# Weight differences and residual adds of a fast-matrix-product FFN stage, moved from GpSimd to VectorE

## The chip, the cores and the metric

The kernel runs on one core of one Trainium2 chip. The metric is the device time of one execution in microseconds (us); each time quoted for a kernel is a median of several runs, and beside it there is one profiled execution with its trace. TensorE runs the matrix products, VectorE (DVE in the rows) and ScalarE (ACT) do elementwise work and can read PSUM, GpSimd (POOL) does elementwise work on SBUF only, SyncE (SP) issues the DMAs. PEld in the rows is TensorE's weight load.

## The reference

One decoder layer: RMS norm, forgetting attention with an output product, a residual add, RMS norm, a SwiGLU feed-forward block, a residual add, and a final RMS norm. What matters here is the end:

```python
def swiglu(h, w_in, w_out):
    gate, up = jnp.split(h @ w_in, 2, axis=-1)
    return ((jax.nn.silu(gate) * up) @ w_out).astype(h.dtype)
...
    h = h + swiglu(rms_norm(h, ffn_norm[i]), ffn_w_in[i], ffn_w_out[i])
h = rms_norm(h, final_norm)
return h[:, N_META:]
```

`h` here is 1024 x 1024 (the 16 meta rows are not needed any more), the hidden width is 2816, and all is float32.

## The kernel before

**The second product of the feed-forward block** (`... @ w_out`) is the last stage. It is a 2 x 2 block product done with seven block products in place of eight (Strassen-Winograd): the hidden activations are cut in four blocks of 512 rows by 1408, the weights `w2` in four blocks of 1408 by 512. The sums of activation blocks (`s1` to `s4`) were made in the stage before by `hidden_sums` and lie in DRAM; the differences of weight blocks are made in this stage, in place:

- t1 = w12 - w11, written over w11 (`to_t1`, line 1015)
- t2 = w22 - t1, written over w11 again (`to_t2`, line 1028)
- t3 = w22 - w12, written over w12 (`to_t3`, line 1036)
- t4 = w21 - t2, written over w21 (`to_t4`, line 1054)

The seven products run in the order a11, a12, s1, s2, s3, s4, a22. Each has 11 steps over the inner dimension (`h` in `prod2`), each step 4 row blocks (`i`), and each of those 3 matmuls (lines 945 to 947): every float32 operand is split into a high and a low part of a format that TensorE takes, and high x high, high x low and low x high are added in PSUM. So a step is 12 matmuls of 128 x 128 by 128 x 512, a product 132.

**What feeds a step.** `left` (line 938) loads the 128 x 512 activation tile by SP's queue into one of four `rm` buffers, and `split` (lines 735 to 740) makes the two parts: ScalarE casts the high part, VectorE subtracts it for the low part. The weight tile is split in the same way. The parts lie in pools `wh` and `wl` of eight buffers each; a step takes two of each, so splits can be four steps ahead of TensorE and no more. `load_w` loads weight tiles, one with each step, put behind the latest `left` load in SP's queue. In s1 to s4 a call `ahead(h)` makes the weight difference of step `h` before its split; the aliases `wt` and `rt` (lines 962 and 963) both are GpSimd's `tensor_tensor`. Of a22's 11 steps the last eight (`TM`) are ordered by row block, with the weight parts in tiles of their own (`t4h` in the buffer of tag `xh`, `t4l`).

**What takes the products away.** `prod2` returns four PSUM banks. They alternate between two sets of four, so a product's banks are wanted again by the product after the next. a11 is copied to `x1` by ScalarE (line 1009) and a12 is added to it by VectorE into `c11` (line 1012); s1 is copied to `p5` by ScalarE (line 1021); s2 is added to `x1`, from then on `u2` (line 1033); s3 + u2 gives `u3` (line 1041); s4 is added to u2 (line 1059); a22 is added to u3 at the very end (line 1082). Residual rows of `h` come from DRAM (`residual`, line 965): a load into one of three `wraw` buffers, then an add on GpSimd (line 968). There are 16 of them, four for each quarter of the output. `square_sum` (line 972, ScalarE) makes the sums for the last norm; GpSimd multiplies c11 and p5 by the gain `gob` (lines 1026 and 1051); `finish` scales and stores.

**Order.** The program is written in the order above, and a planner puts the instructions of each engine in one fixed order at build time from its own simulated times (`schedule_with_timeline_sim=True`): an instruction that is ready and has the earliest place in the program goes first. On the chip each engine keeps that order; an instruction that waits holds what is behind it. SP's queue is in order too.

Of the kernel before, what the change touches and what calls it, by code (L numbers as in the profile page):

```python
# [11 lines left out]
ALU = mybir.AluOpType  # L12
# [3 lines left out]
D = 1024  # L16
# [6 lines left out]
NHP = NHT // 2  # L23
EPS = 1e-6
# [11 lines left out]
def fox_block(ctx, tc, hT, hN, wqkvg, w0f, w0g, wo, w1, w2, g_attn, g_ffn, g_fin, g_q, g_k, b_f, out):  # L36
    nc = tc.nc
# [81 lines left out]
    def t512(tag, name, dt=F32):  # L119
        return ap_.tile([P, 512], dt, tag=tag, name=name, bufs=BUFS[tag])  # L120
# [4 lines left out]
    xh = [xhb[:, k] for k in range(NK)]  # L125
# [609 lines left out]
    def split(src, name):  # L735
        hi = wp.tile([P, 512], F32R, tag="wh", name=f"{name}h", bufs=8)
        lo = wp.tile([P, 512], F32R, tag="wl", name=f"{name}l", bufs=8)
        nc.scalar.copy(hi, src)
        nc.vector.tensor_tensor(lo, src, f32v(hi), ALU.subtract)
        return hi, lo  # L740
# [14 lines left out]
    tt = nc.vector.tensor_tensor  # L755
# [134 lines left out]
    def block(tag, name):  # L890
        if tag in ("V", "K"):
            if not spare.get(tag):
                t = ap2.tile([P, 2, 512], F32, tag=tag, name=name, bufs=2)
                spare[tag] = [t[:, 0], t[:, 1]]
            return spare[tag].pop(0)
        return t512(tag, name)

    w11 = [block(g, f"w11_{h}") for h, g in enumerate(["raw"] * 4 + ["tmp"] * 4 + ["V"] * 3)]
    w21 = [block(g, f"w21_{h}") for h, g in enumerate(["sb"] * 8 + ["K"] * 3)]
    wide = {  # L900
        g: big.tile([P, 16, 512], F32, tag=g, name=f"w2{g}")[:, :, :512] for g in ("xh", "xl")
    }
    w12, w22 = ([wide[g][:, h] for h in range(NHP)] for g in ("xh", "xl"))
    x1 = [t512("cmb", f"x1q{i}") for i in range(4)]
    u3 = [wide["xl"][:, NHP + i] for i in range(4)]
    c11, p5 = (
        [v for n in range(2) for v in (lambda t: (t[:, 0], t[:, 1]))(
            ap_.tile([P, 2, 512], F32, tag="Q", name=f"{m}_{n}", bufs=4))]
        for m in ("c11", "p5")
    )  # L910
    gob = [block("K", "go0"), block("V", "go1")]
# [5 lines left out]
    def load_w(blocks, o, d):  # L917

        def go(h):
            def load():  # L920
                nc.sync.dma_start(blocks[h], w2[h + NHP * o, :, 512 * d : 512 * d + 512])

            if queued:
                with tc.issue_after(queued[-1].ins):
                    load()
            else:
                load()

        return go
# [3 lines left out]
    def banks(name):  # L933
        nprod[0] += 1
        tags = ("SSSO", "mmmM")[nprod[0] % 2]
        return [bank(g, f"y{name}_{n}") for n, g in enumerate(tags)]

    def left(name, h):
        g = t512("rm", f"g{name}_{h}")
        queued.append(nc.sync.dma_start(g, gq_d[name][h]))  # L940
        return split(g, f"g{name}_{h}")

    def mm(o, i, h, g, w):
        sl = slice(i * P, (i + 1) * P)
        nc.tensor.matmul(o, lhsT=g[0][:, sl], rhs=w[0], start=(h == 0), stop=False)  # L945
        nc.tensor.matmul(o, lhsT=g[0][:, sl], rhs=w[1], start=False, stop=False)  # L946
        nc.tensor.matmul(o, lhsT=g[1][:, sl], rhs=w[0], start=False, stop=(h == NHP - 1))  # L947

    def prod2(name, n, blocks, upto=NHP, ahead=None, after=None):
        py = banks(n)  # L950
        for h in range(upto):
            g = left(name, h)
            if ahead is not None:
                ahead(h)
            w = split(blocks[h], f"w{n}_{h}")
            for i in range(4):
                mm(py[i], i, h, g, w)
            if after is not None:
                after(h)
        return py  # L960

    wt = nc.gpsimd.tensor_tensor
    rt = nc.gpsimd.tensor_tensor

    def residual(dst, i, c):
        t = wp.tile([P, 512], F32, tag="wraw", name=f"hr{i}_{c}", bufs=3)
        nc.sync.dma_start(t, hd[i, :, 512 * c : 512 * c + 512])
        rt(dst, dst, t, ALU.add)

    def square_sum(ss, c, h, name):  # L970
        sq = t512("cmb", name)
        nc.scalar.activation(sq, h, AF.Square, bias=0.0, scale=1.0, accum_out=ss[:, c : c + 1])

    def sums(i, n):

        shape = [P, NT, 4] if n > 1 else [P, 8]
        t = sm.tile(shape, F32, tag="ssq" if n > 1 else ("ss", "sv", "sr", "sy0")[i], name=f"oss{i}{n}", bufs=2 if n > 1 else 1)
        if n > 1:
            t = t.rearrange("p a b -> p (a b)")
        return t  # L980
# [26 lines left out]
    y = prod2("a11", 1, w11, ahead=load_first)  # L1007
    for i in range(4):
        nc.scalar.copy(x1[i], y[i])
    y = prod2("a12", 2, w21, ahead=load_w(w12, 0, 1))  # L1010
    for i in range(4):
        tt(c11[i], y[i], x1[i], ALU.add)
        residual(c11[i], i, 0)

    def to_t1(h):
        wt(w11[h], w12[h], w11[h], ALU.subtract)
        load_w(w22, 1, 1)(h)

    y = prod2("s1", 5, w11, ahead=to_t1)
    for i in range(4):  # L1020
        nc.scalar.copy(p5[i], y[i])

    ss = sums(0, 4)
    for i in range(4):
# [1 line left out]
        nc.gpsimd.tensor_tensor(c11[i], c11[i], gob[0], ALU.mult)  # L1026

    def to_t2(h):
        wt(w11[h], w22[h], w11[h], ALU.subtract)

    y = prod2("s2", 6, w11, ahead=to_t2)
    for i in range(4):
        tt(x1[i], y[i], x1[i], ALU.add)
    u2 = x1

    def to_t3(h):
        wt(w12[h], w22[h], w12[h], ALU.subtract)

    y = prod2("s3", 7, w12, ahead=to_t3)
    for i in range(4):  # L1040
        tt(u3[i], y[i], u2[i], ALU.add)
        rt(u2[i], u2[i], p5[i], ALU.add)
        residual(u2[i], i, 1)
    for i in range(4):
        rt(p5[i], p5[i], u3[i], ALU.add)
        residual(p5[i], 4 + i, 1)
        residual(u3[i], 4 + i, 0)
    bs = sums(1, 4)
    for i in range(4):
        square_sum(bs, i, p5[i], f"osq{4 + i}_1")  # L1050
        nc.gpsimd.tensor_tensor(p5[i], p5[i], gob[1], ALU.mult)
    nc.vector.tensor_scalar(bs[:, 4:8], bs[:, 0:4], 1.0 / D, EPS, ALU.mult, ALU.add)

    def to_t4(h):
        wt(w21[h], w21[h], w11[h], ALU.subtract)

    y = prod2("s4", 3, w22, ahead=to_t4)
    for i in range(4):
        tt(u2[i], y[i], u2[i], ALU.add)


    TM = 8
    y = prod2("a22", 4, w21, upto=NHP - TM)
    gs, ws = [], []
    his = big.tile([P, 16, 512], F32R, tag="xh", name="t4h")[:, :, :512]
    los = [t512(g, f"t4l{n}", F32R) for n, g in enumerate((["raw"] * 4 + ["tmp"] * 4)[:TM])]
    for n in range(TM):
        h = NHP - TM + n
# [71 lines left out]
```

## Time and profile before

| | |
|---|---|
| time, median of 3 runs | 1428.16 us (1428.06 to 1429.14) |
| the profiled execution: its time | 1425.88 us |
| the profiled execution: its span | 1424.2 us, 20704 instructions |
| busy in the span: TensorE | 1375.4 us, 97% |
| VectorE | 1017.0 us, 71% |
| ScalarE | 661.9 us, 46% |
| GpSimd | 466.6 us, 33% |
| HBM traffic | 124 GB/s over the span |

Times in the profile are microseconds from the start of the span. Busy times of TensorE come from modelled ends of pipelined matmuls, so a gap between two starts shows a stall better than the busy share does. Waits are inferred from semaphore events and put down to the one that came last.

### The profile page before, as it was taken

What the parts mean: (1) busy time and instruction counts of PE and PEld (TensorE: products, weight loads), DVE (VectorE), ACT (ScalarE), POOL (GpSimd) and SP (SyncE); (2) the same over time, 40 slices, a digit from 0 to 9 for tenths busy, and PEclk for the clock granted to TensorE, in tenths of its full rate; (3) what the DMA queues carried; (4) which work ended last, traced back from release to release, by engine and by line L of the source; (5) the groups of instructions that cost most, each with busy time, mean ns of one, the idle gap of its engine ahead of it and who ended that gap; (6) DMA issues with size and microseconds to landing.
All of it is one profiled execution on the core that took longest, in us unless ns stands there. A gap on an engine that the chain in (4) does not pass through costs nothing.

```text
span 1424.2 us, 20704 instructions
## 1 busy us (share of the span) xinstructions
PE 1375.4 (97%) x6699; PEld 1113.3 (78%) x6699; DVE 1017.0 (71%) x1796; ACT 661.9 (46%) x1428; POOL 466.6 (33%) x724
## 2 busy tenths in 40 slices
PE   7999999999999999999997999999999999999997
PEld 7897887878786887866676888888888888876875
DVE  7656776776876777755758786666666765799696
ACT  6455555646565556635435333322233324444534
POOL 4012625244251626244404011111111111598091
PEclk9999999999999999999998999999999999999999
DMA  6353436272625345289773142233333228652344
GB/s 203 103 145 95 138 105 172 77 200 73 185 86 135 109 116 177 81 282 359 276 264 126 60 138 106 94 107 111 111 111 112 97 81 310 218 168 89 97 148 155
DMA packets 118526, 207.18 MB, mean 145 GB/s; under 512 B 18057, under 2 KB 27282, under 8 KB 118418
## 3 DMA queue, kind: packets, MB, share of 16 engines
q1 hardware_dynamic: 118418, 205.86, 45.1%
q8 instruction: 53, 0.87, 0.3%
q14 instruction: 55, 0.45, 0.1%
HBM read 125.71 MB, written 50.60 MB: 124 GB/s over the span
## 4 chain that ended last, share of the span: by engine, by line
PE 72%; DVE 12%; DMA 6%; ACT 4%; issue 3%; SPq 3%; POOL 0%; DVEq 0%; ACTq 0%; POOLq 0%
PE f L750 10%; PE f L752 10%; PE f L751 10%; PE pj L196 5%; PE pj L197 5%; PE pj L198 5%; PE O L413 4%; DMA wraw<-wqkvg 3%; PE y L946 3%; PE y L945 3%; PE y L947 3%; PE S L359 2%; PE S L360 2%; DVE rm L381 2%; ACT sb L402 1%
## 5 line engine op out<-in xcount | busy, mean ns | idle before, releaser
L196 PE MATMUL pj<-wh,xhb 128*128 128x384 f32 (+1 forms) x512 | 176.7, 346 | 6.4 <-ACT xhb L147 5.7
L197 PE MATMUL pj<-wl,xhb 128*128 128x384 f32 (+1 forms) x512 | 175.3, 344 | 0.0
L198 PE MATMUL pj<-wh,xlb 128*128 128x384 f32 (+1 forms) x512 | 173.1, 342 | 0.0
L371 POOL TENSOR_SCALAR_AFFINE_SELECT sb<-sb 128x128 f32<-128x128 f32 (+2 forms) x160 | 54.5, 344 | 339.4 <-ACT sb L366 338.9
L366 ACT ACTIVATE sb<-S,nb 128x512 f32<-128x512 f32 (+4 forms) x224 | 116.3, 540 | 69.8 <-POOL gap L426 35.4
L428 POOL TENSOR_TENSOR t<-t,sb 128x512 f32<-128x512 f32 (+4 forms) x160 | 140.4, 877 | 4.1
L829 POOL TENSOR_TENSOR gs<-u,u 128x512 f32<-128x512 f32 x11 | 14.2, 1292 | 370.9 <-DVE u L816 370.9
L381 DVE TENSOR_TENSOR rm<-rm,sb 128x512 f32<-128x512 f32 (+4 forms) x160 | 103.2, 645 | 36.1 <-POOL sb L371 17.6
L401 DVE TENSOR_TENSOR sb<-sb,pb 128x512 f32<-128x512 f32 (+4 forms) x224 | 95.8, 497 | 35.6 <-PE pb L395 34.1
L402 ACT ACTIVATE sb<-sb 128x512 f32<-128x512 f32 (+4 forms) x224 | 95.2, 482 | 43.8 <-DVE sb L401 43.8
L196 PEld LDWEIGHTS pj<-wh,xhb 128*128 128x128 f32 x512 | 97.6, 191 | 15.6 <-ACT xhb L147 5.7
L197 PEld LDWEIGHTS pj<-wl,xhb 128*128 128x128 f32 x512 | 97.8, 191 | 1.3
L198 PEld LDWEIGHTS pj<-wh,xlb 128*128 128x128 f32 x512 | 97.2, 190 | 1.2
L413 PE MATMUL O<-sb,V 128*64 128x512 f32 (+4 forms) x448 | 94.4, 464 | 1.1 <-ACT sb L402 1.1
L359 PE MATMUL S<-Q,K 128*128 128x512 f32 (+4 forms) x224 | 76.5, 344 | 0.4 <-ACT sb L366 0.4
L360 PE MATMUL S<-Q,K 128*128 128x512 f32 (+4 forms) x224 | 72.5, 328 | 0.0
L413 PEld LDWEIGHTS O<-sb,V 128*64 128x64 f32 (+1 forms) x448 | 32.9, 135 | 35.9 <-issue 20.4
L106 DVE TENSOR_TENSOR wl<-wraw,wh 128x512 fp32r<-128x512 f32 x56 | 43.8, 788 | 22.8 <-ACT wh L104 21.2
L796 DVE TENSOR_TENSOR u<-f,x 128x512 f32<-128x512 f32 x19 | 13.1, 691 | 62.0 <-PE f L752 62.0
L104 ACT CAST wh<-wraw 128x512 fp32r<-128x512 f32 (+1 forms) x64 | 38.6, 607 | 37.9 <-DMA wraw<-wqkvg 26.4
L359 PEld LDWEIGHTS S<-Q,K 128*128 128x128 f32 (+1 forms) x224 | 39.1, 175 | 19.5 <-ACT sb L366 8.0
L451 PE MATMUL pg<-xhb,wh 128*128 128x512 f32 x112 | 45.1, 403 | 0.4 <-DVE tk L308 0.3
(1382 smaller groups left out, 3879.2 us busy)
## 6 DMA issues: line engine op xcount, KB each, us to landing
Q<-tq SPq DMA_DIRECT2D x128, 128.0 KB, 2.3
wraw<-wqkvg SPq DMA_DIRECT2D x56, 256.0 KB, 4.2
av<-w SPq DMA_DIRECT2D x22, 512.0 KB, 3.2
gs<-qs SPq DMA_DIRECT2D x44, 256.0 KB, 2.6
ga<-qa SPq DMA_DIRECT2D x33, 256.0 KB, 3.8
K<-tk SPq DMA_DIRECT2D x64, 128.0 KB, 2.7
wowh<-wod SPq DMA_DIRECT2D x32, 256.0 KB, 5.5
wowl<-wod SPq DMA_DIRECT2D x32, 256.0 KB, 5.7
```

What stands on the lines that cost most here:

```text
L196: nc.tensor.matmul(o, lhsT=xh[k][:, sl], rhs=wh, start=(k == 0), stop=False)
L197: nc.tensor.matmul(o, lhsT=xh[k][:, sl], rhs=wl, start=False, stop=False)
L198: last_mm[0] = nc.tensor.matmul(o, lhsT=xl[k][:, sl], rhs=wh, start=False, stop=(k == NK - 1))
L359: nc.tensor.matmul(psx[:n, s0:], lhsT=kk[:, j * P : j * P + n], rhs=q[:, 0, s0:], start=True, stop=False)
L366: nc.scalar.activation(sj, psx[:n, s:], AF.Identity, bias=nbias[c][:n, j, head : head + 1], scale=1.0)
L381: nc.vector.tensor_tensor(rm[:n, s:], rm[:n, s:], sj, ALU.max)
L402: nc.scalar.activation(sj, sj, AF.Exp, bias=0.0, scale=1.0)
L413: nc.tensor.matmul(po[r, s:], lhsT=st["V"][:n, j, r], rhs=sj, start=(i == 0), stop=(i == nt - 1))
L428: nc.gpsimd.tensor_tensor(total[e][:n, s:], src[:n, s:], sj, ALU.add)
L750: nc.tensor.matmul(pp, lhsT=s[0][:, ks], rhs=bh, start=(k == 0), stop=False)
L751: nc.tensor.matmul(pp, lhsT=s[0][:, ks], rhs=bl, start=False, stop=False)
L752: nc.tensor.matmul(pp, lhsT=s[1][:, ks], rhs=bh, start=False, stop=(k == 3))
```

## The change

All four weight differences go from GpSimd to VectorE (`tt` is VectorE's `tensor_tensor`). `residual` gets a source: the add reads a product from PSUM together with the loaded rows and writes to SBUF, on VectorE. The residual of the first quarter is added to a11 (into c11) and a12 then to that sum; the residuals of the two right-hand quarters are added to s1, in two results: `p5` as before and the new `p5u`, which lies in four free slots of the buffer that holds w12 (rows of 2048 bytes per slot); ScalarE's four copies of s1 go. The add of p5u to u2, of u3 to p5, and of the last residual to u3 go to VectorE and to later places. What stays on GpSimd in this stage are the eight multiplies by `gob`.

```diff
-    wt = nc.gpsimd.tensor_tensor
-    rt = nc.gpsimd.tensor_tensor
-    def residual(dst, i, c):
+    def residual(dst, src, i, c):
         t = wp.tile([P, 512], F32, tag="wraw", name=f"hr{i}_{c}", bufs=3)
         nc.sync.dma_start(t, hd[i, :, 512 * c : 512 * c + 512])
-        rt(dst, dst, t, ALU.add)
+        tt(dst, src, t, ALU.add)
...
     y = prod2("a11", 1, w11, ahead=load_first)
     for i in range(4):
         nc.scalar.copy(x1[i], y[i])
+        residual(c11[i], y[i], i, 0)
     y = prod2("a12", 2, w21, ahead=load_w(w12, 0, 1))
     for i in range(4):
-        tt(c11[i], y[i], x1[i], ALU.add)
-        residual(c11[i], i, 0)
+        tt(c11[i], y[i], c11[i], ALU.add)
     def to_t1(h):
-        wt(w11[h], w12[h], w11[h], ALU.subtract)
+        tt(w11[h], w12[h], w11[h], ALU.subtract)
         load_w(w22, 1, 1)(h)
     y = prod2("s1", 5, w11, ahead=to_t1)
+    p5u = [wide["xh"][:, NHP + i] for i in range(4)]
     for i in range(4):
-        nc.scalar.copy(p5[i], y[i])
+        residual(p5u[i], y[i], i, 1)
+        residual(p5[i], y[i], 4 + i, 1)
...
     def to_t2(h):
-        wt(w11[h], w22[h], w11[h], ALU.subtract)
+        tt(w11[h], w22[h], w11[h], ALU.subtract)
...
     def to_t3(h):
-        wt(w12[h], w22[h], w12[h], ALU.subtract)
+        tt(w12[h], w22[h], w12[h], ALU.subtract)
     y = prod2("s3", 7, w12, ahead=to_t3)
     for i in range(4):
         tt(u3[i], y[i], u2[i], ALU.add)
-        rt(u2[i], u2[i], p5[i], ALU.add)
-        residual(u2[i], i, 1)
+    def to_t4(h):
+        tt(w21[h], w21[h], w11[h], ALU.subtract)
+    y = prod2("s4", 3, w22, ahead=to_t4)
     for i in range(4):
-        rt(p5[i], p5[i], u3[i], ALU.add)
-        residual(p5[i], 4 + i, 1)
-        residual(u3[i], 4 + i, 0)
+        tt(u2[i], u2[i], p5u[i], ALU.add)
+        tt(u2[i], y[i], u2[i], ALU.add)
+    TM = 8
+    y = prod2("a22", 4, w21, upto=NHP - TM)
     bs = sums(1, 4)
     for i in range(4):
+        tt(p5[i], p5[i], u3[i], ALU.add)
+        residual(u3[i], u3[i], 4 + i, 0)
         square_sum(bs, i, p5[i], f"osq{4 + i}_1")
         nc.gpsimd.tensor_tensor(p5[i], p5[i], gob[1], ALU.mult)
...
-    def to_t4(h):
-        wt(w21[h], w21[h], w11[h], ALU.subtract)
-    y = prod2("s4", 3, w22, ahead=to_t4)
-    for i in range(4):
-        tt(u2[i], y[i], u2[i], ALU.add)
-    TM = 8
-    y = prod2("a22", 4, w21, upto=NHP - TM)
```

## Rows read from the trace of the kernel before

**Rows 1.** The page: busy time, share of the span, instructions of each engine.
```profile
PE 1375.4 (97%) x6699; PEld 1113.3 (78%) x6699; DVE 1017.0 (71%) x1796; ACT 661.9 (46%) x1428; POOL 466.6 (33%) x724
```
**Rows 2.** Timeline of TensorE: first matmul of products a12 to a22, and the last.
```profile
1223.52 0.39 PE L945 MATMUL y<-w_0h,ga_0h 128*128 128x512 f32 x1
...
1253.44 0.39 PE L945 MATMUL y<-w_0h,gs_0h 128*128 128x512 f32 x1
...
1286.35 0.39 PE L945 MATMUL y<-w_0h,gs_0h 128*128 128x512 f32 x1
...
1321.71 0.39 PE L945 MATMUL y<-w_0h,gs_0h 128*128 128x512 f32 x1
...
1351.63 1.07 PE L945 MATMUL y<-w_0h,gs_0h 128*128 128x512 f32 x4
...
1383.56 0.39 PE L945 MATMUL y<-w_0h,ga_0h 128*128 128x512 f32 x1
...
1416.73 0.39 PE L947 MATMUL y<-t4h,ga_10l 128*128 128x512 f32 x1
```
**Rows 3.** Windows, one for each product a12 to a22: span, busy us (instructions), clock, DMA.
```profile
1223.52:1253.44 29.92, 29.92 (x134) 24.77 (x132) 23.05 (x23) 13.08 (x25) 17.40 (x13) 1.00 0.60 194
1253.44:1286.35 32.91, 31.45 (x134) 24.39 (x132) 30.66 (x24) 16.25 (x33) 32.91 (x20) 1.00 0.46 144
1286.35:1321.71 35.36, 32.35 (x134) 24.15 (x132) 33.82 (x29) 13.07 (x25) 25.68 (x16) 1.00 0.32 99
1321.71:1351.63 29.92, 29.92 (x134) 24.78 (x132) 20.14 (x33) 16.54 (x31) 0.21 (x1) 1.00 0.31 89
1351.63:1383.56 31.93, 30.83 (x133) 24.52 (x132) 31.93 (x23) 12.88 (x26) 31.93 (x19) 1.00 0.47 146
1383.56:1416.96 33.40, 31.54 (x133) 24.06 (x131) 24.84 (x46) 17.79 (x42) 8.68 (x6) 1.00 0.49 168
```
**Rows 4.** Timeline of TensorE inside a step of s2: what it waited for.
```profile
1306.75 0.39 PE L945 MATMUL y<-w_6h,gs_6h 128*128 128x512 f32 x1
1307.52 0.50 PE L946 MATMUL y<-w_6l,gs_6h 128*128 128x512 f32 x1 [0.39 <-DVE w_6l L739]
```
**Rows 5.** Timeline of VectorE, late in s2.
```profile
1310.79 1.78 DVE L739 TENSOR_TENSOR gs_8l<-gs,gs_8h 128x512 fp32r<-128x512 f32 x1
1312.49 0.68 DVE L739 TENSOR_TENSOR w_8l<-w,w_8h 128x512 fp32r<-128x512 f32 x1
1313.10 0.68 DVE L739 TENSOR_TENSOR gs_9l<-gs,gs_9h 128x512 fp32r<-128x512 f32 x1
```
**Rows 6.** Timeline of GpSimd: its last instructions in s2.
```profile
1303.48 8.55 POOL L1055 TENSOR_TENSOR w<-w,w 128x512 f32<-128x512 f32 x5
```
**Rows 7.** By line: VectorE's adds of a12 from PSUM (min/median/max ns, first and last start).
```profile
L1012 DVE TENSOR_TENSOR c<-y,x1q x4: 675/676/678, 1253.4 to 1256.3; 128x512 f32<-128x512 f32 x4
```
**Rows 8.** Groups of GpSimd by line, 1210 to 1425: count, busy us, mean ns, idle before.
```profile
L1029 POOL TENSOR_TENSOR w<-w2xl,w 128x512 f32<-128x512 f32 x11 | 19.1, 1740 | 0.0
...
L1016 POOL TENSOR_TENSOR w<-w2xh,w 128x512 f32<-128x512 f32 x11 | 16.0, 1469 | 21.1 <-DMA w2xh<-w 17.7 <-DVE w_3l L739 1.6 <-issue 1.0
...
L1026 POOL TENSOR_TENSOR c<-c,w 128x512 f32<-128x512 f32 x4 | 6.9, 1735 | 0.0
```
**Rows 9.** Waits from 1200 us on: us in total, times, longest.
```profile
ACT osq L972 <- POOL c L968: 12.1, 4, 4.8
```
**Rows 10.** Timeline of SP's queue early in s1.
```profile
1253.53 0.32 SPq L940 DMA_DIRECT2D gs<-qs  x1
...
1259.35 0.32 SPq L967 DMA_DIRECT2D hr<-hd  x1
1259.76 0.38 SPq L940 DMA_DIRECT2D gs<-qs  x1
```
**Rows 11.** By line: from issue to landing, residual loads (line 967).
```profile
DMA to landing us min/median/max: 2.6/3.0/6.4
```
**Rows 12.** By line: from issue to landing, weight loads (line 921).
```profile
DMA to landing us min/median/max: 2.6/4.0/6.9
```

## The prediction

> **What bounds the kernel now.** I read the page first: TensorE is busy 97% of the span [rows 1], so only stalls of TensorE are to be had. The change touches the last stage alone, so I went to the timeline of TensorE there and took the first matmul of each product [rows 2]. Products a12 and s3 take 29.92 us each, 132 matmuls at 0.2267 us: TensorE without a stall. The others take longer: s1 32.91 (2.99 over), s2 35.36 (5.44 over), s4 31.93 (2.01 over), and a22 33.40 from its first matmul to 0.23 us behind the start of its last (3.48 over). The sum of the excess is 13.92 us. The clock column is 1.00 in all six windows [rows 3], so this is waiting and not a slower clock.
>
> What it waits for stands inside a step [rows 4]: the first matmul of step 6 of s2 starts at 1306.75, the second only at 1307.52 in place of 1306.98, released by VectorE's low part of the weights. One step of s2 needs two such splits. VectorE starts them 1.70 us apart (1310.79 to 1312.49) and then, from 1312.49 on, 0.61 apart [rows 5]; in between GpSimd's last weight difference ends, at 1303.48 + 8.55 = 1312.03 [rows 6]. So the same instruction on the same kind of tile costs 1.70 us beside GpSimd and 0.60 without it. Two at 1.70 are 3.40 us a step, and TensorE needs 2.72 (29.92 / 11). That is why the excess stands where GpSimd is busy through the window and VectorE too: s1, s2, s4 have GpSimd at 32.91, 25.68, 31.93 us; in s3 it has 0.21 and there is no excess [rows 3]. a22 inherits emptied buffers from s4. In a12 GpSimd works 17.40 us, with breaks, and the buffers hold.
>
> A second path has the same source. The square sums of c11 waited 12.1 us for GpSimd's residual adds [rows 9], and ScalarE's casts stand behind them in its order; SP's queue stood from 1253.53 to 1259.35 until such an add freed a `wraw` buffer, with the next activation load behind it [rows 10].
>
> **The change part by part.**
>
> *GpSimd loses 44 differences and 16 residual adds, and 8 adds of u2 and p5.* What it keeps is 4 + 4 multiplies by the gain (1.735 us each beside VectorE [rows 8]). The gain of this part is bounded by 13.92 us, since TensorE's matmuls stay as they are, 924 of them.
>
> *VectorE takes the 44 differences.* No row shows one on VectorE. The nearest is the split itself, also two SBUF inputs and one output of 128 x 512: 0.60 us pitch alone, 1.70 beside GpSimd [rows 5]; these are the bounds, and I take 0.60 but for what the eight multiplies disturb. The inputs at multiples of 2048 bytes are no other case: the weight tiles that are split in s3 are slots of the same kind, and s3 has VectorE at 20.14 us for 33 instructions with no excess [rows 3]. Each of the products s1 to s4 gets 11 of them: 11 x 0.60 = 6.6 us.
>
> *VectorE takes residual adds and the adds of u2, p5, u3.* With a source in PSUM the bound below is a12's add, 0.676 us, measured while GpSimd was busy [rows 3, 7]: such an add does not slow beside GpSimd. I take 0.60 of pitch for all. Counts per product after the change, old splits included: s1 22 splits + 11 differences + 4 adds = 37; s2 22 + 11 + 8 = 41; s3 37; s4 22 + 11 + 4 + 4 = 41; a22 22 + 12 = 34 and the small work of the norm. At 0.60: 22.2, 24.6, 22.2, 24.6, 20.4 us, each under TensorE's 29.92. a12 has 26 (15.6 us), and differences may move up into it once w12 is there.
>
> *The eight multiplies stay and collide.* Each takes one VectorE instruction from 0.60 to 1.70: 1.1 us, 8.8 us in all, 4.4 in one product. On s2 that is 24.6 + 4.4 = 29.0, still under 29.92 but with nothing to spare. The Trainium skill ("SBUF — State Buffer", section "Who interferes with whom") says that a Vector instruction with two SBUF inputs and a GpSimd one that reads SBUF block each other, the later one wholly; the 1.70 to 0.60 step agrees. By full blocking for GpSimd's 1.735 us the eight would cost 13.9 us.
>
> *The adds that are moved, and the queues.* 16 residual loads remain 16, 0.32 us of SP each [rows 10]; four go ahead of a12's loads, eight from behind s3 to behind s1, past the loads of s2 and s3. They land in 3.0 us [rows 11] and have three buffers: of the eight adds behind s1 three find their rows there, and two more rounds of three each wait for landing and add, about 1.8 + 2 x 3.6 = 9 us. What stands behind them on VectorE are the splits of s2; four steps of finished splits are a cover of 10.9 us. The banks of s1 are held 9 us in place of some 2.5, and are wanted by s3, 29.92 us later: nothing. ScalarE loses four copies that were not on the path: nothing. The buffer of `t4h` now comes free only after u2 + p5u; the eight casts and subtractions that fill it then may gather at the start of a22, where the last eight steps want them 8.2 us (three steps) in.
>
> *A wait that is new.* A difference whose weights come late made GpSimd wait, 17.7 us in line 1016 [rows 8], at no cost. On VectorE such a wait holds the splits. Weight loads land in 4.0 us, 6.9 at most [rows 12]. Bounds: nothing, where the planner puts the difference behind the landing; or up to the spread of 2.9 us at some steps, under the cover of 10.9 as long as it does not recur at each step.
>
> **Sum.** 13.92 us of excess, less what I leave: nothing in s1, s3, s4; 1 us in s2 (29.0 of 29.92 in VectorE, the eight adds); 1 us in a22 (its multiplies, `t4h`). That is 12 us. Of the profiled execution's 1425.88 it leaves 1413.9; the median of the runs is 2.28 us above that execution, so I forecast 1428.16 - 12 = 1416.2 us (-0.84%).
>
> **The rivals.**
>
> *Crowding.* The waits go, but s2 or a22 keeps an excess, because the eight adds stand as one block with their loads or because `t4h`, the splits and u2, u3, p5 gather at the start of a22. For it: 29.0 of 29.92, and a22's 3.48 us today. Against: 74% load over the six products (15.6 + 22.2 + 24.6 + 22.2 + 24.6 + 24 with the norm = 133 of 179.5 us) leaves room to run ahead. Price 3 to 7 us more: about 1420 (1418.5 to 1423).
>
> *The loads hold VectorE.* If 11 differences of t1 and 11 of t3 each wait 1 us more, that is 11 us in each of a12 and s1, beside 15.6 to 24.6 of work: 26.6 to 35.6 against 29.92, and most of the gain is gone: 1425.3 to 1430. For it: line 1016's waits [rows 8]. Against: the loads run a product ahead.
>
> *VectorE becomes the bound: slower.* s1 to s4 hold 156 VectorE instructions in 119.7 us; at a pitch of 0.77 they fill it, and at (119.7 + 13.9) / 156 = 0.86 all of today's excess is back. With the multiplies' 8.8 us I have 0.656. If in-order waits for ScalarE's casts and for loads bring the mean to 0.90, TensorE loses 140.4 - 133.6 = 6.8 us against today: 1435. For it: VectorE is at 93 to 100% of its windows in s1, s2, s4 [rows 3]. Against: that share is made of 1.70s. The Trainium skill ("Perfetto Trace Analysis", section "Optimizing Scalar/DVE Operations") says to move work away from a saturated VectorE, to GpSimd if need be, which would speak for this rival; it adds that the two share a port and that this may not help, and the rows decide for the second.
>
> **Chances.** Forecast 0.60 (its own range 1413.5 to 1418.5), crowding 0.25, loads 0.08, VectorE the bound 0.07. Nothing below 1428.16 - 13.92 = 1414.2 but for the scatter between runs. About 0.2% (2.9 us) is what a measurement of this kernel tells from no change. Faster by more: 0.60 + 0.25 = 0.85; within: 0.08; slower: 0.07. The range takes in the forecast and crowding, 85%: 1413 to 1423.
>
> **What would show it.** In the profile after: splits of s1, s2, s4 at 0.68 us except beside the eight multiplies; GpSimd near empty from a12 on; first matmuls of s2, s3, s4, a22 29.9 us apart; no square sum waiting for GpSimd. Crowding shows as a gap at the second to fourth step of s2 or of the last eight steps of a22; late loads as VectorE idle before a difference, released by a DMA. I would be wrong if a difference on VectorE took clearly over 0.7 us with GpSimd idle, or if the planner set differences or adds ahead of splits that TensorE wants sooner.

## The result and the profile after

The changed kernel takes 1419.28 us (median of 6 runs, 1416.00 to 1424.52), the kernel before 1429.05 beside it (6 runs, 1428.06 to 1432.30): a ratio of 0.9931 [0.9917, 0.9946], 9.8 us less. The forecast was 12 us less, 1416.2; 1419.28 lies in the stated range (1413 to 1423), but above the forecast's own (1413.5 to 1418.5).

The page's busy times, which answer to [rows 1]: GpSimd falls from 466.6 to 361.1 us, and VectorE falls too, from 1017.0 to 995.4, though it has 68 instructions more.

```profile
PE 1372.7 (97%) x6699; PEld 1116.0 (79%) x6699; DVE 995.4 (70%) x1864; ACT 659.9 (47%) x1424; POOL 361.1 (25%) x656
```

The first matmuls of a12, s1, s3, s4 and a22 and the last of all, on TensorE's timeline, answer to [rows 2]; at the seam of s1 and s2 two matmuls change places, so these two are taken as a pair.

```profile
1225.99 0.39 PE L945 MATMUL y<-w_0h,ga_0h 128*128 128x512 f32 x1
...
1255.91 0.39 PE L945 MATMUL y<-w_0h,gs_0h 128*128 128x512 f32 x1
...
1315.76 0.39 PE L945 MATMUL y<-w_0h,gs_0h 128*128 128x512 f32 x1
...
1345.67 0.39 PE L945 MATMUL y<-w_0h,gs_0h 128*128 128x512 f32 x1
...
1381.30 0.39 PE L945 MATMUL y<-w_0h,ga_0h 128*128 128x512 f32 x1
...
1410.99 0.39 PE L947 MATMUL y<-t4h,ga_10l 128*128 128x512 f32 x1
```

s1 and s2 take 59.85 us together, twice 29.92; a12, s3 and a22 take 29.92 each. Only s4 is over: 1345.67 to 1381.30 are 35.63 us, 5.71 too many. The windows of s1 to a22 (columns as in [rows 3]):

```profile
1255.91:1285.83 29.92, 29.92 (x133) 24.77 (x132) 29.92 (x46) 14.90 (x30) 6.13 (x4) 1.00 0.42 132
1285.83:1315.76 29.93, 29.93 (x134) 24.78 (x133) 22.60 (x38) 12.61 (x23) 0.00 (x0) 1.00 0.59 178
1315.76:1345.67 29.91, 29.91 (x133) 24.77 (x132) 16.54 (x27) 12.55 (x23) 0.00 (x0) 1.00 0.34 97
1345.67:1381.30 35.63, 32.43 (x133) 25.68 (x132) 32.18 (x48) 19.00 (x39) 11.24 (x4) 0.95 0.30 89
1381.30:1411.22 29.92, 29.92 (x133) 24.59 (x131) 16.56 (x39) 15.59 (x37) 0.00 (x0) 1.00 0.45 161
```

VectorE is busy for all of s1 and TensorE loses nothing there: differences were pulled forward. Of the 44, by the starts in the trace, 5 run in a11, 14 in a12, 23 in s1 and 2 in s2, so s1's 46 instructions are partly work of s2, s3 and s4; s2 and s3 have 38 and 27. s4 has 48, none of them a difference, and its clock is not 1.00. All of TensorE's waits from 1250 us to the end (us in total, times, longest) lie in s4:

```profile
PE y L946 <- DVE w_7l L739: 2.3, 1, 2.3
PE y L946 <- DVE w_4l L739: 0.6, 1, 0.6
PE y L946 <- DVE w_6l L739: 0.2, 1, 0.2
```

VectorE's timeline in s4 shows what stood ahead of those splits. L1047 adds p5u to u2, L1068 makes `t4l`, L1059 is the norm's small work on 128 x 4:

```profile
1348.40 1.56 DVE L1047 TENSOR_TENSOR x1q<-x1q,w2xh 128x512 f32<-128x512 f32 x1
...
1352.29 1.78 DVE L1047 TENSOR_TENSOR x1q<-x1q,w2xh 128x512 f32<-128x512 f32 x1
...
1354.59 0.68 DVE L1047 TENSOR_TENSOR x1q<-x1q,w2xh 128x512 f32<-128x512 f32 x1
...
1355.79 1.78 DVE L739 TENSOR_TENSOR gs_4l<-gs,gs_4h 128x512 fp32r<-128x512 f32 x1
...
1361.71 1.88 DVE L1068 TENSOR_TENSOR t4l<-w,t4h 128x512 fp32r<-128x512 f32 x3
1363.51 0.68 DVE L739 TENSOR_TENSOR w_6l<-w2xl,w_6h 128x512 fp32r<-128x512 f32 x1
1364.11 3.09 DVE L1068 TENSOR_TENSOR t4l<-w,t4h 128x512 fp32r<-128x512 f32 x5
1367.12 1.24 DVE L1059 TENSOR_SCALAR oss<-oss 128x4 f32<-128x4 f32 x1
1368.28 0.68 DVE L739 TENSOR_TENSOR gs_7l<-gs,gs_7h 128x512 fp32r<-128x512 f32 x1
1368.88 0.68 DVE L739 TENSOR_TENSOR w_7l<-w2xl,w_7h 128x512 fp32r<-128x512 f32 x1
```

The splits of step 7 come behind all eight of `t4l`, which no matmul reads before 1389.7, in a22 (the view by tile):

```profile
L946 PE MATMUL y<-t4l,ga_3h x4: 389/389/389, 1389.7 to 1406.0; 128*128 128x512 f32 x4
```

Four of VectorE's instructions take 1.24 to 1.78 us; beside each stands one of GpSimd's four multiplies of p5 (GpSimd's timeline):

```profile
1348.11 1.29 POOL L1058 TENSOR_TENSOR p<-p,w 128x512 f32<-128x512 f32 x1 [84.38 <-ACT osq L969]
1351.99 1.52 POOL L1058 TENSOR_TENSOR p<-p,w 128x512 f32<-128x512 f32 x1 [2.59 <-ACT osq L969]
1355.56 1.46 POOL L1058 TENSOR_TENSOR p<-p,w 128x512 f32<-128x512 f32 x1 [2.04 <-ACT osq L969]
1361.38 6.96 POOL L1058 TENSOR_TENSOR p<-p,w 128x512 f32<-128x512 f32 x1 [4.36 <-ACT osq L969]
```

Each of the four starts while a multiply is under way, and ends 0.55 us behind its end (1349.96 behind 1349.40, 1354.07 behind 1353.51, 1357.57 behind 1357.02) or, the small one on 128 x 4, with it (1368.36 and 1368.34).

And TensorE's timeline behind its longest wait: from 1370.15 to 1373.13 matmuls start 0.43 us apart in place of 0.23.

```profile
1366.19 1.07 PE L945 MATMUL y<-w_7h,gs_7h 128*128 128x512 f32 x4
1369.61 0.74 PE L946 MATMUL y<-w_7l,gs_7h 128*128 128x512 f32 x1 [2.35 <-DVE w_7l L739]
1370.15 0.63 PE L947 MATMUL y<-w_7h,gs_7l 128*128 128x512 f32 x1
1370.58 0.63 PE L946 MATMUL y<-w_7l,gs_7h 128*128 128x512 f32 x1
...
1373.13 1.08 PE L945 MATMUL y<-w_8h,gs_8h 128*128 128x512 f32 x4
```

The window 1369.50 to 1373.00 has a granted clock of 0.53, near the lower level of 1.2 GHz. So s4 has two losses: waits of 0.60, 0.25 and 2.35 us, and a slow stretch that followed the longest.

### The profile page after: what moved, and what is told of

The parts are those of the page before. It is cut to its first block, busy times and chain, and to the rows that moved or that the text cites. A ratio compares the mean times of both kernels' runs of the same rounds, so it can differ in the third digit from the quotient of the medians.

```text
span 1418.4 us, 20660 instructions
## 1 busy us (share of the span) xinstructions
PE 1372.7 (97%) x6699; PEld 1116.0 (79%) x6699; DVE 995.4 (70%) x1864; ACT 659.9 (47%) x1424; POOL 361.1 (25%) x656
```

## The experiments

The table gives each run's time and, worked out from TensorE's timeline of its profile, the last stage: from the second matmul of s1 to the second of s3 (s1 and s2), from there to the last matmul (s3 to a22), and both. Executions reach s1 up to 8 us apart (1253.66 in the profile of before, 1261.50 at the latest). They are that far apart at a11's first matmul already (1193.60 and 1201.44), with the same order of instructions on every engine ahead of it; the length from s1 on is therefore the sharper measure, and the median of the runs the check on it. It comes from one profiled execution of each row.

| kernel | median us (range, runs) | ratio to before [95%] | s1, s2 | s3 to a22 | both |
|---|---|---|---|---|---|
| before | 1429.05 (1428.06 to 1432.30, 6) | 1 | 68.28 | 94.79 | 163.07 |
| after | 1419.28 (1416.00 to 1424.52, 6) | 0.9931 [0.9917, 0.9946] | 59.84 | 95.01 | 154.85 |
| differences on GpSimd | 1430.33 (1426.38 to 1433.38, 12) | 0.9998 [0.9988, 1.0009] | 68.79 | 95.09 | 163.88 |
| differences only | 1423.76 (1421.78 to 1425.59, 5) | 0.9954 [0.9941, 0.9967] | 63.01 | 94.73 | 157.74 |
| no p5 multiply | 1416.40 (1414.56 to 1419.99, 5) | 0.9910 [0.9896, 0.9923] | 59.84 | 89.34 | 149.18 |
| p5u in own buffers | 1414.64 (1413.89 to 1415.66, 4) | 0.9894 [0.9882, 0.9907] | 59.84 | 89.31 | 149.15 |
| slots of 2064 bytes | 1419.68 (1418.45 to 1425.44, 8) | 0.9922 [0.9902, 0.9943] | 59.84 | 95.01 | 154.85 |
| differences thrice | 1435.33 (1432.35 to 1438.75, 10) | 1.0031 [1.0015, 1.0047] | 72.18 | 95.86 | 168.04 |
| own buffers, diff. on GpSimd | 1425.80 (1420.79 to 1428.70, 10) | 0.9963 [0.9945, 0.9981] | 68.60 | 89.31 | 157.91 |
| p5 multiply on VectorE | 1419.82 (1419.77 to 1421.28, 5) | 0.9928 [0.9903, 0.9953] | 59.84 | 91.68 | 151.52 |
| after, again | 1419.91 (1418.31 to 1423.15, 4) | 0.9930 [0.9908, 0.9951] | 59.84 | 93.45 | 153.29 |
| p5 on VectorE, again | 1418.42 (1417.17 to 1419.66, 4) | 0.9913 [0.9892, 0.9935] | 59.84 | 91.70 | 151.54 |
| own buffers, again | 1416.09 (1414.96 to 1418.05, 4) | 0.9901 [0.9883, 0.9920] | 59.85 | 89.30 | 149.15 |
| own buffers, p5 on VectorE | 1416.51 (1415.07 to 1419.02, 4) | 0.9905 [0.9884, 0.9925] | 59.84 | 89.30 | 149.14 |

The kernel before, on the same chips, had medians of 1429.73 beside the first four experiments, 1430.53 beside the next three, 1429.56 beside the one after and 1430.02 beside the last four. 149.15 is the floor: 658 intervals of 29.92 / 132 us, without a wait. Before is 13.92 above it, after 5.70.

**Differences back on GpSimd.** In `to_t1` to `to_t4` of the changed kernel:

```diff
-        tt(w11[h], w12[h], w11[h], ALU.subtract)
+        nc.gpsimd.tensor_tensor(w11[h], w12[h], w11[h], ALU.subtract)
```

> The 44 weight differences go back to GpSimd, all else as in the changed kernel. Shared-port theory (a GpSimd instruction with two SBUF inputs takes VectorE's splits from 0.60 to 1.70 us): s1 and s2 get back most of their 8.4 us of excess, 5 to 9 us, and s4 keeps its 5.7: 1424 to 1429 us. Rival, held queues (what cost time was ScalarE's and SP's queues standing behind GpSimd's residual adds, 12.1 us of waiting square sums): the differences matter little, s1 and s2 stay within 1 us of 29.92 each, 1419 to 1421 us.

1430.33 us, no difference from before, and a little above the 1424 to 1429 expected; the stage is 9.03 us longer than the changed kernel's. The windows of s1 and s4:

```profile
1255.10:1288.90 33.80, 31.91 (x134) 24.39 (x132) 33.80 (x24) 15.45 (x32) 33.80 (x21) 1.00 0.35 111
...
1353.80:1389.50 35.70, 32.48 (x133) 25.68 (x132) 32.11 (x48) 18.98 (x39) 11.27 (x4) 0.95 0.30 91
```

s1 has GpSimd busy throughout again, and s1 and s2 are back at 68.79 us. s4 stays as in the changed kernel. So the moved adds alone bring nothing, the rival of the held queues falls, and s4's excess is the adds' and not the differences'.

**The differences only.** The kernel before with one line changed:

```diff
-    wt = nc.gpsimd.tensor_tensor
+    wt = nc.vector.tensor_tensor
```

> The kernel before with only the 44 weight differences moved to VectorE; the residual adds stay on GpSimd as they were. Shared-port theory: s1 and s2 fall from 8.4 us of excess to 0 to 2, since GpSimd has eight instructions there in place of some 40; s4 and a22 keep their 5.5 us, with 20 GpSimd instructions there: 1420 to 1423 us. Held queues: the waits of the square sums and of SP stay, and so does most of the excess, 1426 to 1430 us.

1423.76 us; the stage loses 5.33 of its 13.92 us of excess, all in s1 and s2. What is left there, 63.01 - 59.84 = 3.17 us where 0 to 2 was expected, stands in s1 beside GpSimd's residual adds and c11 multiplies (TensorE's waits):

```profile
PE y L946 <- DVE w_4l L739: 1.1, 1, 1.1
...
PE y L946 <- DVE w_5l L739: 0.7, 1, 0.7
```

From s3 on it is the kernel before. The adds are thus worth 3.17 us in s1, but only once the differences are gone from GpSimd: what each part is worth in s1 and s2 depends on which is moved first (differences 5.27 with the adds left, 8.95 with the adds moved).

**Without the p5 multiplies.** The changed kernel leaves out the multiply of p5 by the final gain, so the lower right quarter of the output lacks that gain.

```diff
-        nc.gpsimd.tensor_tensor(p5[i], p5[i], gob[1], ALU.mult)
```

> The changed kernel without GpSimd's four multiplies of p5 by the final gain (that gain is left out of the lower right quarter of the output). Shared-port theory: in s4 these four cost VectorE some 4.2 us (three instructions of 1.56 to 1.78 us, and 1.24 us for a 128 x 4 one), and TensorE's 3.2 us of waits in s4, with the half clock of 3.4 us behind them, go: s4 at 29.9 to 31 us, 1413.5 to 1415.5 us. Rival, VectorE's own crowd (u2, p5, u3 and eight subtractions of t4l stand ahead of the splits of steps 6 and 7): s4 keeps 3 us or more of excess, 1417 to 1420 us.

1416.40 us, 0.9 above the range expected; TensorE waits nowhere in the stage, and s4 is where it was expected. Its window of s4:

```profile
1345.90:1375.80 29.90, 29.90 (x133) 24.75 (x132) 27.88 (x48) 19.28 (x38) 0.00 (x0) 1.00 0.39 107
```

The same 48 VectorE instructions, eight of `t4l` among them, now take 27.88 us and fit. The split of `w_7l` starts 18.82 us behind the second matmul of s4, in the changed kernel 22.98: the four multiplies cost VectorE 4.16 us. So do the four slow instructions taken one by one: 0.88, 1.10, 1.10 and 1.08 us over their 0.68 and 0.16 here.

**p5u in buffers of its own.** The changed kernel with p5u out of the buffer whose place `t4h` takes:

```diff
-    p5u = [wide["xh"][:, NHP + i] for i in range(4)]
+    p5u = [t512(g, f"p5u{i}") for i, g in enumerate(("sb", "sb", "cmb"))] + [wide["xl"][:, NHP + 4]]
```

> The changed kernel with p5u in four other free buffers, so that the buffer of t4h comes free at the last split of w12 and the eight casts and subtractions of t4l are ahead of s4's splits, as in the kernel before. Both the shared-port and the crowd theory: 4.8 us of VectorE leave s4's early steps, the wait before step 7 goes and the half clock with it: s4 at 29.9 to 30.7 us, 1413.5 to 1415.5 us, with less scatter than the 8.5 us from fastest to slowest of the changed kernel. Rival, the clock falls there of itself: s4 keeps 1.7 us and the scatter stays. Rival, the eight subtractions now delay s3: s3 over 29.92 by 1 us or more.

1414.64 us, the fastest kernel of all, and no wait of TensorE in the stage though the multiplies are back. The view by tile gives the eight casts into `t4h` in the changed kernel:

```profile
L1067 ACT CAST t4h<-w x8: 613/615/617, 1355.9 to 1360.1; 128x512 fp32r<-128x512 f32 x8
```

and the view by line the same in this one:

```profile
L1067 ACT CAST t4h<-w x8: 612/616/620, 1336.2 to 1339.9; 128x512 fp32r<-128x512 f32 x8
```

In the changed kernel the first cast follows the last of the p5u adds (1354.59 + 0.68 = 1355.27) and lies in s4. Here all eight lie in s3, as in the kernel before (1342.7 to 1346.4, s4 from 1351.63). GpSimd's multiplies now stand beside VectorE for 19.36 us of s4, and nothing waits:

```profile
1345.10:1375.10 30.00, 30.00 (x134) 24.82 (x134) 28.38 (x42) 15.89 (x33) 19.36 (x4) 1.00 0.40 115
```

The edit moved more than `t4h`: GpSimd's four multiplies of c11 went, from s1 (1256.46) into s2 (from 1292.05), where TensorE does not wait either.

**Slots at multiples of 2064 bytes.** The two wide buffers of the changed kernel:

```diff
-        g: big.tile([P, 16, 512], F32, tag=g, name=f"w2{g}")[:, :, :512] for g in ("xh", "xl")
+        g: big.tile([P, 15, 516], F32, tag=g, name=f"w2{g}")[:, :, :512] for g in ("xh", "xl")
```

> The changed kernel with its wide slots at multiples of 2064 bytes instead of 2048. Theory (the places of the buffers play no part): the difference takes 0.68 us at a pitch of 0.60 as before, the product s4 is again the only one over 29.92 us, 1416 to 1424 us. Rival (the multiples of 2048 bytes matter): the two-input operations or the transfers of the last stage change their durations, and the time leaves 1414 to 1426 us.

1419.68 us. The same three waits of TensorE, the same 154.85 us, and a difference (L1028) takes 673 to 689 ns for 674 to 684. The multiple of 2048 plays no part.

**Each difference three times.** In `to_t1` to `to_t3` of the changed kernel; three subtractions in place end where one does:

```diff
-        tt(w11[h], w12[h], w11[h], ALU.subtract)
+        for _ in range(3):
+            tt(w11[h], w12[h], w11[h], ALU.subtract)
```

> The changed kernel with each difference of s1, s2 and s3 done three times on VectorE, which leaves the result as it is up to rounding; 22 more VectorE instructions in each of the three products. Theory (VectorE has room for 49 instructions at 0.60 us in a product of 29.92 us, and becomes the bound beyond them): 59, 63 and 59 instructions take 35.4, 37.8 and 35.4 us, so s1 to s3 together lose about 19 us, less what was done ahead of them (up to 6 us); about 1432 to 1439 us. Rival (the remainder of the changed kernel comes from GpSimd and from late buffers alone, and VectorE is never near its limit): under 1423 us.

1435.33 us, slower than before: VectorE is the bound now. s2's window and GpSimd's timeline:

```profile
1289.20:1330.40 41.20, 34.06 (x132) 26.26 (x132) 41.20 (x65) 13.38 (x23) 10.75 (x4) 0.92 0.40 122
```

```profile
1264.82 35.14 POOL L1026 TENSOR_TENSOR c<-c,w 128x512 f32<-128x512 f32 x4 [58.69 <-ACT osq L969]
```

66 more instructions cost the stage 168.04 - 154.85 = 13.2 us; the forecast was 19 less up to 6, so it holds at its lower edge. Some 2.4 us of it are not VectorE's directly: behind TensorE's wait for `w_1l` in s2 twelve matmuls start 0.43 us apart, and the window 1296.20 to 1303.00 has a granted clock of 0.50.

**Own buffers, with the differences on GpSimd.** Both edits shown above together.

> The changed kernel with the differences back on GpSimd and the p5u products in buffers of their own. Theory (two causes that add: the differences on GpSimd cost s1 and s2 about 9 us, the late buffer of t4h costs s4 about 5.7 us): s1 and s2 stay at 68 to 69 us, s4 is at 29.9 us, about 1423 to 1426 us. Rival (the s4 remainder is GpSimd's multiplies, which the differences on GpSimd delay further): s4 keeps 4 us or more, 1427 to 1431 us.

1425.80 us: s1 and s2 at 68.60, s3 to a22 at the floor. The causes add: the buffers give 163.88 - 157.91 = 5.97 us here, and 5.70 with the differences on VectorE. With the run of the differences only, which kept 94.73 us, it also shows that the 5.48 us that the kernel before lost from s3 on (94.79 - 89.31) were its GpSimd adds'.

**The p5 multiplies on VectorE.** In the changed kernel:

```diff
-        nc.gpsimd.tensor_tensor(p5[i], p5[i], gob[1], ALU.mult)
+        nc.vector.tensor_tensor(p5[i], p5[i], gob[1], ALU.mult)
```

> The changed kernel with the four multiplies of p5 by the gain on VectorE in place of GpSimd. Theory (they cost s4 some 4.2 us because they slow VectorE's two-input operations beside them): VectorE pays 4 x 0.60 = 2.4 us for them and nothing is slowed, so its work ahead of the last splits of s4 is 1.8 us shorter, the wait of 2.35 us for w_7l shrinks to under 1 us, and s4 falls from 35.6 to 30 to 32 us; 1414.5 to 1417.5. Rival (it is the count of instructions ahead of the splits that matters and not the sharing): s4 stays at 33 us or more, 1417.5 to 1421.

The split of `w_7l` starts 21.23 us behind s4's second matmul, 1.75 earlier, for the 1.8 expected. The waits for `w_4l` and `w_6l` go, but the one for `w_7l` is 2.08 us and not under 1, and s4 is at 32.30, so 52 instructions with none slowed do not fit either. The stage is 3.33 us shorter than in the changed kernel's profile; the median, 1419.82, showed nothing of it. So it ran again, with three others.

**Four kernels on one chip.** The changed kernel, the p5 multiplies on VectorE, p5u in its own buffers, and the last two edits together.

> The changed kernel as it is, on one chip with the next three. Theory (s4's two waits and its stretch at half clock stand in every execution, and the rest scatters by some us between executions): s4 is the one product over 29.92 us, at 32 to 36 us; 1418 to 1421. Rival (the 5.71 us were one execution's): s4 at 30 us or less.

> The four multiplies of p5 on VectorE once more. Theory (s4 at 32.3 us for the changed kernel's 35.6): again about 32.3 us, and the median 2 to 4 us under the changed kernel's on this chip. Rival (the gain in s4 is one execution's, or is given back in front of the stage): the median within 1.5 us of the changed kernel's.

> The p5u products in buffers of their own once more. Theory: no product over 29.92 us, and the median 3 to 6 us under the changed kernel's on this chip. Rival: within 1.5 us of it.

> Both edits: p5u in buffers of their own and the p5 multiplies on VectorE. Theory (with the buffers alone every product is at 29.92 us, so there is nothing left for the second edit): the same time as with the buffers alone, within 1.5 us. Rival (the multiplies on GpSimd still cost something that the first matmuls of the products don't show, such as a later end): 2 us or more faster.

Against the changed kernel's 1419.91 the medians are 1.5, 3.8 and 3.4 us lower. The stage gives 1.75, 4.14 and 4.15, so stage and time agree. The second was expected 2 to 4 lower and is at 1.5, the edge of its rival; only its stage, the same twice, speaks for it. The two edits together bring nothing over the buffers alone.

The changed kernel's s4 was 34.06 us this time and not 35.63, so the expectation that the half clock stands in every execution fell. It had the same wait, but without a slow stretch behind it (TensorE's timeline; its window 1374.20 to 1377.70 has a clock of 1.00):

```profile
1374.23 0.50 PE L946 MATMUL y<-w_7l,gs_7h 128*128 128x512 f32 x1 [2.35 <-DVE w_7l L739]
1374.57 0.39 PE L947 MATMUL y<-w_7h,gs_7l 128*128 128x512 f32 x1
```

So of the 5.71 us 4.14 are the waits and the slower start behind each, in both executions, and 1.57 the slow stretch of one of them.

## Why the prediction was right, and where it failed

- **TensorE's excess of 13.92 us was all there was to gain, and it was waiting for splits slowed by GpSimd.** Right. With p5u in its own buffers no wait is left, and beside before on the same chips the kernel is 15.1 and 13.9 us faster. Of it the differences are 8.95 us, in s1 and s2 (68.79 to 59.84), once the adds are moved. The prediction's second path, square sums and SP's queue behind GpSimd's adds, brought nothing by itself: with it gone and the differences on GpSimd, s1 and s2 stayed at 68.79. (SP's queue stood from 1254.32, not 1253.53: a weight load stands between.)
- **A difference on VectorE at 0.60 us pitch.** Right: 42 of the 44 took 0.67 to 0.70 us, and the two beside a multiply of c11 1.19 and 1.78. That each of s1 to s4 gets eleven was not so: 19 ran in a11 and a12, 23 in s1, 2 in s2.
- **The remainder: 1 us in s2, 1 us in a22, nothing in s1, s3, s4.** This step failed. s2 and a22 keep nothing, and s4 keeps 4.14 us, in one execution 5.71. The forecast of 12 us less was 2.2 us too good, and this term, 2 us where 4.14 stayed, is of that size: 13.92 - 4.14 = 9.78, where the medians fell by 9.77. That it meets to 0.01 is luck: the other profile leaves 13.92 - 5.70 = 8.22.
- **Why it failed.** Both causes were named, both in the wrong product. `t4h`'s buffer does come free only after u2 + p5u, but its casts and subtractions do not wait for a22: they start at 1355.9, 0.6 us behind the last reader, in the middle of s4. The eight adds of p5 + u3 and of the last residual rows, counted for a22, run in s4 too. So s4 has 48 VectorE instructions and not 41, though none of its eleven differences is left in it; with `t4l` out of it, it has 42. And the p5 multiplies, priced at 4.4 us and measured at 4.16, run in s4, not in a22. 48 x 0.60 + 4.16 is 33 us against 29.92. Either cause alone fits; each was taken away alone, and s4 fell to the floor both times.
- **The prediction's sign of being wrong** (differences or adds ahead of splits that TensorE wants sooner) came true with other work: the eight of `t4l`, first read at 1389.7, stand ahead of the splits of step 7, for which TensorE waited until 1369.61. By estimate, their 8 x 0.60 = 4.8 us put behind those splits would start `w_7l`'s 18.2 us into s4, and 18.82 was early enough without the multiplies. So the planner's order may be a third cause that is needed for the loss; no run changed the order alone, and this is not shown.
- **The adds from s3 on.** The prediction took 2.01 + 3.48 us of s4 and a22 as gained but for 1 us. They were gained (5.48 us) and lost again to the new crowding (5.70): s3 to a22 take 95.01 us after and 94.79 before, and 93.45 in the execution without the slow stretch. Nearly all that the change shows is s1 and s2.
- **Eight residual adds behind s1, with three buffers.** Nothing, as said: they lie between the splits, and TensorE does not wait in s2.
- **Rival: crowding.** This came, in size (1418.5 to 1423) and kind, but not at either of the places named. It had 0.25, and the forecast's own range 0.60: that the time lies in the stated range is owed to this rival, not to the sum.
- **Rival: the loads hold VectorE.** Fell. `to_t1` waited 3.2 us in four instructions for its weights, `to_t3` 1.5 in three, and TensorE for none. (Its upper bound, 35.6, took s2's 24.6 us of work; a12 and s1 have 15.6 and 22.2, so it is 33.2.)
- **Rival: VectorE the bound.** Not here: its busy share of 29.92 in s1 is work done ahead. But the bound is close. 22 instructions more in each of three products made the kernel slower than before.
- **The multiplies' price, 1.1 us each.** Right: 1.04. Each slowed instruction ended 0.55 us behind its multiply or with it, so VectorE paid what was left of the multiply when it came, not the whole. The other way round, GpSimd's four multiplies of c11, which took 6.1 us in the changed kernel, took 35.14 beside the differences done three times, one of them 30.54. The Trainium skill ("SBUF — State Buffer", section "Who interferes with whom") says that the one that comes second is blocked wholly; both directions agree. The prediction's 13.9 us for eight by that rule charged VectorE a whole 1.735 us [rows 8] each time, as if it always came at the multiply's start.

Open: why the same wait of 2.35 us was followed by a slow stretch in one execution of the changed kernel and not in another. No experiment was made on it. Open too: whether s4 fits by the order of VectorE's work alone.

## What to carry to other kernels

When work moves to a new buffer, ask what used that place next: here a result parked in a free corner put eight casts from 8.9 us ahead of s4 to 10.2 us behind its start, into the one product that had no room for them, and that cost all that the moved adds had gained from s3 on. Two loads that fit alone (48 instructions, 4.16 us of sharing) did not fit together, so count each engine per product with the work that dependencies allow there, not where the program writes it, and look in the order of its work for what is wanted late but stands early. Where an engine slows its neighbour, the neighbour's time drops when it takes over the work: VectorE did 68 instructions more in 22 us less.

## What was not expected of the hardware

- After the wait of 2.35 us TensorE's clock was granted at 0.53 for some 3.4 us in the changed kernel, at 0.54 in the same place with slots of 2064 bytes, at 0.50 (1379.20 to 1382.50) with the differences on GpSimd, and at 1.00 when the changed kernel ran again; behind the wait of 2.08 us (p5 multiplies on VectorE) it was 1.00 in both executions. The stretch cost 1.57 us in the changed kernel.
- A GpSimd multiply of 128 x 512 took 1.29 us at its fastest here and 6.96 at its slowest beside VectorE's two-input operations; in the kernel with p5u in its own buffers up to 10.57.
- VectorE's small operation on 128 x 4 took 1.24 us beside such a multiply and 0.16 without it.
- A run of VectorE's instructions with two SBUF inputs, each starting 0.60 us behind the one before and taking 0.68, let no multiply of GpSimd's through: the last multiply in s4 stood 6.96 us beside such a run, and one stood 30.54 us with each difference done three times. That one ended, at 1295.36, 1.21 us behind the start of VectorE's first add with a source in PSUM (1294.15).
